# Order of the delta rule's 64x64 products, and how two convolution states are loaded and turned

## The chip, the cores and the metric

The kernel runs on one core of a Trainium2 chip. The metric is the device time of one execution, in microseconds (us). A core has five engines that work beside each other, each through its own list of instructions in order: TensorE (PE in the profile; its weight loads are PEld), VectorE (DVE), ScalarE (ACT), GpSimd (POOL) and SyncE (SP), whose queue issues all of this kernel's DMAs.

## What is computed

One decoder layer, for a prompt of 512 tokens and a group of 8 samples with one token each, with a model width of 1024. An input projection feeds two groups of heads beside each other: sparse attention and a gated delta rule. One output projection, a norm, a feed-forward network with a causal convolution of width 3, a second norm, a per-layer embedding and a third norm follow. The change touches the delta rule and the states of the two convolutions. Cut to these, the reference is:

```python
qkv, new_gbuf = causal_dwconv(h[..., C_GQKV:C_GA], gdn_buf, gdn_conv_w)
...
# gated_delta_chunked: chunks of 64 tokens, 8 heads of 64
X = lax.linalg.triangular_solve(A, rhs, left_side=True, lower=True)
val, kcd = X[..., :D], X[..., D:]
inner = jnp.einsum('nbhid,nbhjd->nbhij', q, k) * dec_incl
...
def step(S, xs):
    val_c, kcd_c, inner_c, qg_c, kend_c, gl = xs
    vn = val_c - jnp.einsum('bhcd,bhde->bhce', kcd_c, S)
    o = jnp.einsum('bhcd,bhde->bhce', qg_c, S) + jnp.einsum('bhij,bhje->bhie', inner_c, vn)
    S = S * jnp.exp(gl)[..., None, None] + jnp.einsum('bhcd,bhce->bhde', kend_c, vn)
    return S, o
...
hg, new_fbuf = causal_dwconv(up[..., :D_FF], ffn_buf, ffn_conv_w)
```

`causal_dwconv` puts the state's rows ahead of the new ones: 3 rows of 1536 features per sample for the delta rule, 2 rows of 2816 features per sample for the feed-forward network. Only the samples have such states; the prompt starts from zeros.

## The kernel before, in words

Activations lie feature-major: a tile holds 128 features as partitions and 520 tokens as columns (512 of the prompt, 8 samples), in two halves of 256 and 264 columns. A dense product (`product`, L299 to L307) goes over 8 tiles of the contraction with three matmuls each, since both operands are kept as a high and a low part: high weights by high activations (L303), low by high (L304), high by low (L307). `wtile` loads the weights into one of two buffers named raw (L192) and splits them, with ScalarE for the high part wh (L208) and DVE for the low one wl (L209). Those are the groups that fill the profile.

The delta rule's inputs come first. `gdn_tile` makes one tile of 128 of the 1536 features: a dense product into cb, then the convolution as a multiplication (L419) and pairs of multiply-adds on DVE, one for the prompt (L421), one for the samples (L422) with the state gst as operand. `vectors` (L332, L333) turns rows of parameters into per-feature columns at the first tile, and `conv_state` loads and turns a third of the state at every fourth one: a load of 24 rows (8 samples by 3) of 512 features (L352), four transposes on PE (L355) into one PSUM bank, a copy (L356).

The delta rule itself goes over four tiles tt of 128 tokens, each of two chunks c of 64. PE's array is used in quarters here: products of 64x64 whose contraction runs over one half of the partitions (rows) and whose result lands on one half of the output partitions (columns). A product's place is given by both halves.

- `gdn_pre(tt)` makes what needs no state: val (L667, rows c, columns c), kcd (L676, rows c, columns hp, the head's parity), and qk (L691, rows hp, columns c), each with 16 products, the last two with a PSUM bank per c and per hp.
- `gdn_step(tt, c)` goes from state to state: vn (L708), a subtraction per hp (L711), the new state's products S (L717), an addition (L719).
- `gdn_post(tt)` makes the output: o1 (L732, rows hp, columns c, a bank per hp) from queries and the state ahead of each chunk, o2 (L740), a norm over the heads, and transposes back to features (L751).

Within-chunk products kk (L536, L538) stand ahead of all that, in quarters that are 32 columns wide: four such tiles alternate.

The kernel keeps eight PSUM banks in four pools, `BANKS = dict(mm=2, pg=2, pc=1, pn=3)`. `gdn_pre` takes all of its banks from the two of pg; o1 and o2 use pn. The name of a tile in the profile is that of its PSUM tile: L732 shows as o, L691 as qk.

The program is written in stages whose order the text `ORDER` gives (G0, G1 ... are the delta rule's, D the input projections, F the feed-forward state, N0 and N1 the halves of the first norm, Y the output projection). A list scheduler then orders the instructions of each engine anew: it takes what it holds to be ready, earlier code first.

`ffn_state` is stage F. It stands among the last stages of attention, at some 375 to 397 us, and loads the feed-forward state in six loads of 16 rows (8 samples by 2) of up to 512 features (L1300), each turned by up to four transposes (L1303) and copied (L1304). Six tiles st16 and six PSUM banks of pg pass through it:

```python
for c0 in range(0, NFT, 4):
    n = min(4, NFT - c0)
    st = UV("st16", [16, 512])
    nc.sync.dma_start(st[:, :n * 128], I["state_ffn_conv"][0].rearrange("b r c -> (b r) c")[:, c0 * 128:(c0 + n) * 128])
```

Around it stand attention's last transposes (L940) and products (L947, L948), and the first norm of the first half: mean (L1176), subtraction (L1180), squares (L1182), variance (L1188).

Of the kernel before, what the change touches and what calls it, by code (L numbers as in the profile page):

```python
# [20 lines left out]
T = 512  # L21
# [80 lines left out]
def body(tc, nc, ctx, I, O, dbg=None):  # L102
# [51 lines left out]
    # activations that need a table, in an order that changes tables seldom  # L154
# [31 lines left out]
    # ---- dense products  # L186
# [47 lines left out]
    # ---- tokens to feature-major, in two f32r parts  # L234
# [13 lines left out]
    # the tensor engine's clock rises while the first rows come  # L248
# [39 lines left out]
    def by_halves(name, hv, tag, dt=F32, tiles=8):  # L288
        """tiles of one half, two to a slot"""
# [20 lines left out]
    def dense(specs, rh, rl, order=None, tags=("mm",), where=("w",), extra=None, ws=None, low=None):  # L310
        """specs: (parts, KT, M, evac); the first halves of all, then the second ones."""
# [13 lines left out]
    # per-feature vectors, by transposes of their rows  # L325
# [16 lines left out]
    # ---- delta-rule inputs: convolution, silu  # L342
# [4 lines left out]
    gst = UV("gst", [128, 12, 24])  # L347
    gstv = gst.rearrange("p j (b r) -> p j b r", r=3)

    def conv_state(hf):  # L350
        st = UV("st24", [24, 512])
        nc.sync.dma_start(st, I["state_gdn_conv"][0].rearrange("b r c -> (b r) c")[:, hf * 512:(hf + 1) * 512])  # L352
        ps = PS("gstT", "pn")
        for j in range(4):
            PE.transpose(ps[:, j * 24:(j + 1) * 24], st[:, j * 128:(j + 1) * 128], ident[:24, :24])  # L355
        V.tensor_copy(gst[:, hf * 4:(hf + 1) * 4, :], r3(ps[:, :96], 4))  # L356
# [4 lines left out]
    def gates():  # L361
# [6 lines left out]
        # both parts of the few columns in one operand  # L368
# [27 lines left out]
    def last_rows(rows, nt, outs, c0):  # L396
        """the last tokens' columns of nt tiles, turned and written"""
# [10 lines left out]
    def gdn_tile(j, ws=None):  # L408
# [6 lines left out]
        if j % 4 == 0:  # L415
            conv_state(j // 4)
# [17 lines left out]
    def l2norm(js):  # L434
        """rows of the heads scaled to unit length (queries with the softmax-like factor)"""
# [77 lines left out]
    # ---- within-chunk matrices, inverse of the unit triangular one  # L513
# [86 lines left out]
    # ---- delta rule of the samples, one token each  # L600
# [41 lines left out]
    # ---- delta rule over the chunks  # L642
# [5 lines left out]
    def gdn_pre(tt):  # L648
# [21 lines left out]
        p["kcd"] = U("kcd")  # L670
        for c in range(2):
            q = slice(c * 64, c * 64 + 64)
            pc = PS("kcd", "pg")
            for h in range(8):
                ht, hp = h // 2, h % 2
                PE.matmul(pc[hp * 64:hp * 64 + 64, ht * 64:ht * 64 + 64], kbg[q, h * 64:h * 64 + 64], TTt[q, h, :], start=True, stop=True)  # L676
            S.copy(p["kcd"][:, c * 256:c * 256 + 256], pc[:, :256])
# [906 lines left out]
```

## Time and profile before

| | us |
|---|---|
| median of 3 runs | 897.41 |
| lowest, highest | 895.09, 898.21 |
| span of the profiled execution | 892.7 |
| busy: PE, DVE, ACT, POOL | 859.2, 580.6, 426.6, 192.2 |
| DMA, mean | 96 GB/s |

The profiled execution is shown by its span alone, from the first to the last instruction; what lies around it is not shown. An engine's busy time is the union of its instructions' times. On PE a pass overlaps the next ones, so a short pause of PE hides in the end of a pass before, and two groups of matmuls are compared by the times at which passes start. An fp32 matmul shows as two passes, a matmul of the split type and a transpose as one. "Granted clock" is the share of TensorE's full clock of 2.4 GHz that it was granted: 1.00 is 2.4 GHz and 0.50 is 1.2 GHz.

### The profile page before, as it was taken

The numbers are of one execution on the slowest core, as the hardware profiler recorded it, in microseconds if no ns is written. First come the engines' busy times: TensorE is split into PE (matmuls) and PEld (weight loads), VectorE is DVE, ScalarE is ACT, GpSimd is POOL, SyncE is SP. The second block draws the span as 40 slices with busy tenths as digits, with TensorE's granted clock in tenths as the row PEclk, the third lists the DMA queues.
The fourth block names the chain that finished last, engine by engine and source line by source line (L and its number), as shares of the span: only waits on it lengthen the run. The fifth ranks groups of instructions, "written<-read, shape, count | busy, mean of one in ns | idle before, by whom it ended". The sixth has DMA issues, their size and how long they took to land.

```text
span 892.7 us, 19336 instructions
## 1 busy us (share of the span) xinstructions
PE 859.2 (96%) x7696; PEld 801.7 (90%) x7696; DVE 580.6 (65%) x1319; ACT 426.6 (48%) x940; POOL 192.2 (22%) x299
## 2 busy tenths in 40 slices
PE   8799999999998989999999999999999999998995
PEld 6779998988996758979899999999999999998984
DVE  4488996669869787779554553354543345577967
ACT  4364548323457885745644441244431244434744
POOL 0044040345404332206710000000000000005333
PEclk9899999999999999989999999999999999999998
DMA  8421331333237321333413333332343233352202
GB/s 270 116 67 37 104 91 53 109 96 84 68 98 231 94 79 30 104 101 107 118 48 96 96 105 88 94 90 88 88 117 95 60 87 117 93 162 78 95 1 96
DMA packets 137981, 85.92 MB, mean 96 GB/s; under 512 B 8186, under 2 KB 129708, under 8 KB 137844
## 3 DMA queue, kind: packets, MB, share of 16 engines
q1 hardware_dynamic: 137892, 84.70, 32.1%
q8 instruction: 60, 0.98, 0.4%
q14 instruction: 29, 0.24, 0.1%
HBM read 79.48 MB, written 7.36 MB: 97 GB/s over the span
## 4 chain that ended last, share of the span: by engine, by line
PE 81%; DMA 7%; DVE 7%; ACT 3%; issue 1%; POOL 1%; SPq 0%; DVEq 0%; POOLq 0%; ACTq 0%
PE mm L303 20%; PE mm L307 20%; PE mm L304 19%; PE PT L940 2%; DMA out_dram<-in_state_nsa_win_dram 2%; DMA praw<-in_ple_w_gate_dram 1%; DMA raw<-in_ffn_w_down_dram 1%; PE var L1188 1%; PE O L947 1%; PE O L948 1%; DVE wl L209 1%; PE S L904 1%; PE l L451 1%; DMA raw<-in_w_in_dram 1%; PE S L905 1%
## 5 line engine op out<-in xcount | busy, mean ns | idle before, releaser
L209 DVE TENSOR_TENSOR wl<-raw,wh 128x512 fp32r<-128x512 f32 x192 | 135.0, 705 | 147.4 <-ACT wh L208 146.0
L208 ACT CAST wh<-raw 128x512 fp32r<-128x512 f32 x200 | 121.5, 612 | 200.6 <-PE mm L307 151.1
L304 PE MATMUL mm<-x1h,wl 128*128 128x256 f32 (+1 forms) x704 | 198.3, 282 | 1.0 <-POOL wl L209 1.0
L307 PE MATMUL mm<-x1l,wh 128*128 128x256 f32 (+1 forms) x704 | 198.9, 283 | 0.0
L303 PE MATMUL mm<-x1h,wh 128*128 128x256 f32 (+1 forms) x704 | 198.5, 283 | 0.0
L304 PEld LDWEIGHTS mm<-x1h,wl 128*128 128x128 f32 x704 | 132.3, 188 | 1.3 <-POOL wl L209 1.2
L303 PEld LDWEIGHTS mm<-x1h,wh 128*128 128x128 f32 x704 | 132.3, 188 | 0.2 <-ACT wh L208 0.2
L307 PEld LDWEIGHTS mm<-x1l,wh 128*128 128x128 f32 x704 | 132.2, 188 | 0.1
L303 PE MATMUL mm<-xh,wh 128*128 128x256 f32 (+1 forms) x416 | 122.2, 294 | 0.0
L307 PE MATMUL mm<-xl,wh 128*128 128x256 f32 (+1 forms) x416 | 121.1, 291 | 0.4 <-DVE xl L273 0.4
L304 PE MATMUL mm<-xh,wl 128*128 128x256 f32 (+1 forms) x416 | 120.0, 288 | 0.0
L304 PE MATMUL mm<-hhl,wl 128*128 128x256 f32 (+1 forms) x352 | 99.9, 286 | 0.0
L303 PE MATMUL mm<-hhl,wh 128*128 128x264 f32 (+1 forms) x352 | 99.8, 286 | 0.0
L307 PE MATMUL mm<-hhl,wh 128*128 128x256 f32 (+1 forms) x352 | 99.6, 286 | 0.0
L303 PEld LDWEIGHTS mm<-xh,wh 128*128 128x128 f32 x416 | 79.7, 192 | 2.5 <-ACT xh L272 0.6
L307 PEld LDWEIGHTS mm<-xl,wh 128*128 128x128 f32 x416 | 79.7, 192 | 1.5 <-DVE xl L273 0.6
L304 PEld LDWEIGHTS mm<-xh,wl 128*128 128x128 f32 x416 | 79.6, 191 | 0.8 <-issue 0.5
L1343 POOL COPY last<-fcb 128x10 f32<-128x10 f32 x22 | 4.9, 224 | 309.6 <-ACT fcb L1331 298.1
L303 PEld LDWEIGHTS mm<-hhl,wh 128*128 128x128 f32 x352 | 66.8, 190 | 0.2
L304 PEld LDWEIGHTS mm<-hhl,wl 128*128 128x128 f32 x352 | 66.8, 190 | 0.2
L307 PEld LDWEIGHTS mm<-hhl,wh 128*128 128x128 f32 x352 | 66.4, 190 | 0.2
L1202 POOL TENSOR_SCALAR R<-R,vec 128x264 f32<-128x264 f32 (+1 forms) x40 | 31.0, 788 | 47.8 <-ACT x1h L1199 32.5
(442 smaller groups left out, 1866.3 us busy)
## 6 DMA issues: line engine op xcount, KB each, us to landing
raw<-in_ffn_w_up_dram SPq DMA_DIRECT2D x44, 512.0 KB
raw<-in_w_in_dram SPq DMA_DIRECT2D x26, 512.0 KB
raw<-in_w_out_dram SPq DMA_DIRECT2D x32, 256.0 KB
raw<-in_ffn_w_down_dram SPq DMA_DIRECT2D x16, 512.0 KB
pg<-in_cache_nsa_kv_dram SPq DMA_DIRECT2D x16, 256.0 KB
praw<-in_ple_w_gate_dram SPq DMA_DIRECT2D x8, 512.0 KB
raw<-in_ffn_w_down_dram SPq DMA_DIRECT2D x8, 384.0 KB
xr<-in_x_prompt_dram SPq DMA_DIRECT2D x4, 512.0 KB
```

Of the source, the lines that this page charges most:

```text
L208: both = (S.copy(th[:, :k1 - k0, :M], raw[:, k0:k1, :M]), low.tensor_tensor(tl[:, :k1 - k0, :M], raw[:, k0:k1, :M], th[:, :k1 - k0, :M], o ...
L209: low.tensor_tensor(tl[:, :k1 - k0, :M], raw[:, k0:k1, :M], th[:, :k1 - k0, :M], op=ALU.subtract))
L303: PE.matmul(o, hs[k], rh[hv][k], start=(k == ks[0]), stop=False)
L304: PE.matmul(o, ls[k], rh[hv][k], start=False, stop=False)
L307: PE.matmul(o, hs[k], rl[hv][k], start=False, stop=(k == ks[-1]))
L451: PE.matmul(ps, C("bd64"), sq[:, :T], start=True, stop=True)
L904: PE.matmul(ps[:, :wm], q_[:, ts_], kh[:, :wm], start=True, stop=False)
L905: PE.matmul(ps[:, :wm], q_[:, ts_], kl[:, :wm], start=False, stop=True)
L940: PE.transpose(pt[:, g4 * 128:g4 * 128 + 128], P[g4][:, st * 128:st * 128 + 128], ident)
L947: PE.matmul(po, VV[br][:, st, kv, :], pT_[0][:, :512], start=(br == 0 and st == 0), stop=False)
L948: PE.matmul(po, VV[br][:, st, kv, :], pT_[1][:, :512], start=False, stop=(br == 1 and st == tt))
L1202: G.tensor_scalar(r, r, b_, 1.0, op0=ALU.add, op1=ALU.mult)
```

## The change

Two edits, and comments taken out, which shift line numbers by up to 7.

- The loops of kcd, qk and o1 go over heads outside and chunks inside. For kcd that needs both banks at once, and the copies out of PSUM follow both.
- A helper `turned_rows` loads a state as rows of 128 features, so that sample, row and block of features together make the partitions: 288 rows for the delta rule, 352 for the feed-forward network. Up to three loads, three transposes into one PSUM bank, one copy. `conv_state` is called once, at the first tile. The columns of gst and fst stand in another order, so the multiply-adds read them with a stride.

```diff
-    gst = UV("gst", [128, 12, 24])
-    gstv = gst.rearrange("p j (b r) -> p j b r", r=3)
-
-    def conv_state(hf):
-        st = UV("st24", [24, 512])
-        nc.sync.dma_start(st, I["state_gdn_conv"][0].rearrange("b r c -> (b r) c")[:, hf * 512:(hf + 1) * 512])
-        ps = PS("gstT", "pn")
-        for j in range(4):
-            PE.transpose(ps[:, j * 24:(j + 1) * 24], st[:, j * 128:(j + 1) * 128], ident[:24, :24])
-        V.tensor_copy(gst[:, hf * 4:(hf + 1) * 4, :], r3(ps[:, :96], 4))
+    gst = UV("gst", [128, 288])
+    gstv = gst.rearrange("p (b r j) -> p j b r", b=8, r=3)
+
+    def turned_rows(out, src, n, name, tag):
+        st = UV(name, [128, 3, 128])
+        for a_ in range(0, n, 128):
+            m = min(128, n - a_)
+            nc.sync.dma_start(st[:m, a_ // 128], src[a_:a_ + m, :])
+        ps = PS(name + "T", tag)
+        for a_ in range(0, n, 128):
+            m = min(128, n - a_)
+            PE.transpose(ps[:, a_:a_ + m], st[:m, a_ // 128], ident[:m, :m])
+        V.tensor_copy(out, ps[:, :n])
+
+    def conv_state():
+        turned_rows(gst, I["state_gdn_conv"][0].rearrange("b r (j p) -> (b r j) p", p=128), 288, "gst", "pn")
...
         if not F:
             vectors()
-        if j % 4 == 0:
-            conv_state(j // 4)
+            conv_state()
...
-        for c in range(2):
-            q = slice(c * 64, c * 64 + 64)
-            pc = PS("kcd", "pg")
-            for h in range(8):
+        pcd = [PS("kcd", "pg") for c in range(2)]
+        for h in range(8):
+            for c in range(2):
+                q = slice(c * 64, c * 64 + 64)
                 ht, hp = h // 2, h % 2
-                PE.matmul(pc[hp * 64:hp * 64 + 64, ht * 64:ht * 64 + 64], kbg[q, h * 64:h * 64 + 64], TTt[q, h, :], start=True, stop=True)
-            S.copy(p["kcd"][:, c * 256:c * 256 + 256], pc[:, :256])
+                PE.matmul(pcd[c][hp * 64:hp * 64 + 64, ht * 64:ht * 64 + 64], kbg[q, h * 64:h * 64 + 64], TTt[q, h, :], start=True, stop=True)
+        for c in range(2):
+            S.copy(p["kcd"][:, c * 256:c * 256 + 256], pcd[c][:, :256])
...
         pq = [PS("qk", "pg"), PS("qk", "pg")]
-        for c in range(2):
-            t0 = tt * 128 + c * 64
-            for ht in range(4):
+        for ht in range(4):
+            for c in range(2):
+                t0 = tt * 128 + c * 64
                 for hp in range(2):
...
         po1 = [PS("o1", "pn"), PS("o1", "pn")]
-        for c in range(2):
-            q = slice(c * 64, c * 64 + 64)
-            t0 = tt * 128 + c * 64
-            for ht in range(4):
+        for ht in range(4):
+            for c in range(2):
+                q = slice(c * 64, c * 64 + 64)
+                t0 = tt * 128 + c * 64
                 for hp in range(2):
...
-        fst = UV("fst", [128, NFT, 16])
-        for c0 in range(0, NFT, 4):
...
-        FS["v"] = fst.rearrange("p j (b r) -> p j b r", r=2)
+        fst = UV("fst", [128, NFT * 16])
+        turned_rows(fst, I["state_ffn_conv"][0].rearrange("b r (j p) -> (b r j) p", p=128), NFT * 16, "fst", "pg")
+        FS["v"] = fst.rearrange("p (b r j) -> p j b r", b=8, r=2)
```

What the scheduler makes of it shows in the emitted order, at three places. First PE in `gdn_pre` of the first tile, where the products of qk stand between a matmul of another kind (DT) and the products of the state (S); qk_2227 and qk_2228 are the banks of hp 0 and 1, and the sources are the queries' and keys' tiles of the four ht. Before:

```order
L681 MATMUL DT_2222<-kbg_2171,cst 128x512
L691 MATMUL qk_2227<-qkv_1174,qkv_300 64x64
L691 MATMUL qk_2227<-qkv_1249,qkv_375 64x64
L691 MATMUL qk_2227<-qkv_1480,qkv_449 64x64
L691 MATMUL qk_2227<-qkv_1708,qkv_523 64x64
L691 MATMUL qk_2227<-qkv_1174,qkv_300 64x64
L691 MATMUL qk_2227<-qkv_1249,qkv_375 64x64
L691 MATMUL qk_2227<-qkv_1480,qkv_449 64x64
L691 MATMUL qk_2227<-qkv_1708,qkv_523 64x64
L307 MATMUL mm_2415<-xl_16_87,wh_2411 128x256
L717 MATMUL S_2490<-vn_2477,kend_2172 64x64 x8
```

Now, with kcd of the same stage above it (kcd_2186 and kcd_2187 are the banks of the chunks):

```order
L682 MATMUL kcd_2186<-TTa_947,kbg_2156 64x64 x8
L829 MATMUL kvT_2376<-cst,kvf_273_2313 128x128 x2
L845 MATMUL ntok_2387<-cst,kvf_273_2313 8x128
L682 MATMUL kcd_2187<-TTa_947,kbg_2156 64x64 x8
...
L688 MATMUL DT_2207<-kbg_2156,cst 128x512
L698 MATMUL qk_2212<-qkv_1167,qkv_301 64x64 x2
L698 MATMUL qk_2212<-qkv_1242,qkv_376 64x64 x2
L698 MATMUL qk_2212<-qkv_1465,qkv_450 64x64 x2
L698 MATMUL qk_2212<-qkv_1693,qkv_524 64x64 x2
L307 MATMUL mm_2400<-xl_16_87,wh_2396 128x256
L724 MATMUL S_2475<-vn_2462,kend_2157 64x64 x8
```

Within a bank of qk the two chunks now alternate (the x2), where the four ht of one chunk followed each other; the banks still come one after the other. The two banks of kcd still follow each other too.

Second, PE in `gdn_post` of the first tile, with two banks o per hp; Sst_2078 before and Sst_2063 now is the state ahead of the first chunk, Sst_2499 and Sst_2484 that ahead of the second. Before, first the last rows of chunk 0, then those of chunk 1 behind vn:

```order
L732 MATMUL o_311_2562<-Sst_2078,qkv_1708 64x64
L676 MATMUL kcd_2211<-TTa_946,kbg_2171 64x64 x8
...
L708 MATMUL vn_2536<-Sst_2499,kcd_2200 64x64 x8
L732 MATMUL o_310_2561<-Sst_2499,qkv_1174 64x64
L732 MATMUL o_311_2562<-Sst_2499,qkv_1174 64x64
L732 MATMUL o_310_2561<-Sst_2499,qkv_1249 64x64
L732 MATMUL o_311_2562<-Sst_2499,qkv_1249 64x64
```

Now:

```order
L739 MATMUL o_306_2546<-Sst_2063,qkv_1167 64x64
L739 MATMUL o_307_2547<-Sst_2063,qkv_1167 64x64
...
L715 MATMUL vn_2521<-Sst_2484,kcd_2185 64x64 x8
L739 MATMUL o_306_2546<-Sst_2484,qkv_1167 64x64
L739 MATMUL o_307_2547<-Sst_2484,qkv_1167 64x64
L739 MATMUL o_306_2546<-Sst_2063,qkv_1242 64x64
L739 MATMUL o_307_2547<-Sst_2063,qkv_1242 64x64
L739 MATMUL o_306_2546<-Sst_2484,qkv_1242 64x64
L739 MATMUL o_307_2547<-Sst_2484,qkv_1242 64x64
```

Six of the eight products of chunk 0 have moved from ahead of vn to behind it, where both states and both hp alternate.

Third, SP's queue at the feed-forward state (st before, fst now). Before:

```order
L1247 DMA xr_5413<-in_x_prompt_dram 128x2x128
L1300 DMA st_951_5775<-in_state_ffn_conv_dram 16x512
L192 DMA raw_5733<-in_w_out_dram 128x4x128
...
L192 DMA raw_5972<-in_w_out_dram 128x4x128
L1300 DMA st_953_5783<-in_state_ffn_conv_dram 16x512
L1300 DMA st_955_5791<-in_state_ffn_conv_dram 16x512
L1300 DMA st_957_5799<-in_state_ffn_conv_dram 16x512
L1300 DMA st_959_5807<-in_state_ffn_conv_dram 16x512
L1300 DMA st_961_5815<-in_state_ffn_conv_dram 16x256
```

Now:

```order
L1254 DMA xr_5398<-in_x_prompt_dram 128x2x128
L355 DMA fst_5760<-in_state_ffn_conv_dram 128x128 x2
L355 DMA fst_5760<-in_state_ffn_conv_dram 96x128
L192 DMA raw_5718<-in_w_out_dram 128x4x128
```

All loads of the state now stand where the first one stood; six loads of weights lay between the first and the second. On PE the three transposes stand where the first four of 22 stood.

## Rows read from the trace of the kernel before

**Rows 1.** The page: span, and busy time of each engine with its share and instructions

```profile
span 892.7 us, 19336 instructions
PE 859.2 (96%) x7696; PEld 801.7 (90%) x7696; DVE 580.6 (65%) x1319; ACT 426.6 (48%) x940; POOL 192.2 (22%) x299
```

**Rows 2.** Windows (us; busy us and instructions per engine; PEclk; DMA share; GB/s)

```profile
200.00:265.00 65.00, 65.00 (x862) 59.44 (x861) 53.19 (x108) 29.48 (x70) 22.99 (x29) 1.00 0.29 81
265.00:300.00 35.00, 31.71 (x244) 25.23 (x243) 31.32 (x122) 29.72 (x97) 16.97 (x23) 1.00 0.54 165
```

**Rows 3.** Timeline of PE (start, length, instructions, idle before and releaser), qk

```profile
168.95 0.96 PE L691 MATMUL qk<-qkv,qkv 64*64 64x64 f32 x16
169.84 0.39 PE L307 MATMUL mm<-xl,wh 128*128 128x256 f32 x1
```

**Rows 4.** Timeline of PE, kcd

```profile
162.87 0.63 PE L676 MATMUL kcd<-TTa,kbg 64*64 64x64 f32 x15
163.43 0.44 PE L822 MATMUL kvT<-cst,kvf 128*128 128x128 f32 x2
```

**Rows 5.** Windows, instructions of kk alone (PE, PEld, DVE)

```profile
72.95:74.10 1.15, 0.98 (x64) 0.82 (x64) 0.03 (x1) 1.00 0.00 0
```

**Rows 6.** Timeline of PE, the third group of gst

```profile
84.29 0.42 PE L355 MATMUL gstT<-cst,st 24*128 24x24 f32 x4
84.64 0.39 PE L303 MATMUL mm<-xh,wh 128*128 128x256 f32 x1
84.86 0.28 PE L304 MATMUL mm<-xh,wl 128*128 128x256 f32 x1
84.98 0.28 PE L307 MATMUL mm<-xl,wh 128*128 128x256 f32 x1
```

**Rows 7.** Timeline of PE, the first tile's vectors and state

```profile
29.84 0.29 PE L332 MATMUL vec<-cst,vr 114*128 114x114 f32 x1 [4.06 <-DMA vr<-in_ffn_conv_w_dram]
...
30.90 0.59 PE L355 MATMUL gstT<-cst,st 24*128 24x24 f32 x4 [0.45 <-DMA st<-in_state_gdn_conv_dram]
31.42 0.59 PE L307 MATMUL mm<-xl,wh 128*128 128x264 f32 x1
31.81 0.41 PE L303 MATMUL mm<-xh,wh 128*128 128x256 f32 x1
```

**Rows 8.** Timeline of SP's queue at the same place

```profile
29.09 0.30 SPq L352 DMA_DIRECT2D st<-in_state_gdn_conv_dram  x1
29.50 0.40 SPq L192 DMA_DIRECT2D raw<-in_w_in_dram  x1
```

**Rows 9.** Groups by line: busy us, mean ns, idle before with releaser

```profile
L1303 PE MATMUL fstT<-cst,st 16*128 16x16 f32 x22 | 2.5, 236 | 1.4 <-DMA st<-in_state_ffn_conv_dram 1.4
```

**Rows 10.** Timeline of PE around the feed-forward state

```profile
384.75 1.03 PE L940 MATMUL PT<-cst,P 128*128 128x128 f32 x8
...
391.17 0.63 PE L1303 MATMUL fstT<-cst,st 16*128 16x16 f32 x8 [1.40 <-DMA st<-in_state_ffn_conv_dram]
...
400.67 3.29 PE L1188 MATMUL var<-lsq,cst 128*128 128x256 f32 x14 [0.83 <-ACT lsq L1182]
```

**Rows 11.** Timeline of SP's queue there

```profile
374.73 0.41 SPq L1300 DMA_DIRECT2D st<-in_state_ffn_conv_dram  x1
376.92 10.73 SPq L192 DMA_DIRECT2D raw<-in_w_out_dram  x6
387.74 2.31 SPq L1300 DMA_DIRECT2D st<-in_state_ffn_conv_dram  x5
```

**Rows 12.** Windows at the low clock (columns as in rows 2)

```profile
30.60:37.30 6.70, 6.40 (x31) 6.38 (x32) 2.67 (x7) 2.90 (x6) 0.45 (x1) 0.50 0.62 102
392.40:399.10 6.70, 6.70 (x27) 4.84 (x25) 4.29 (x11) 2.82 (x7) 0.00 (x0) 0.50 0.28 82
```

**Rows 13.** Timeline of DVE, the first norm

```profile
398.21 2.74 DVE L1180 TENSOR_TENSOR R<-R,mu 128x256 f32<-128x256 f32 x8 [0.47 <-PE mu L1176]
```

**Rows 14.** Groups by line of DVE, 155 to 265 us

```profile
L711 DVE TENSOR_TENSOR vn<-vb,vn 64x256 f32<-64x256 f32 x16 | 6.7, 417 | 4.0 <-PE vn L708 3.8
```

More of the change, by code (lines that the diff above doesn't have):

```diff
@@ L670, in gdn_pre @@
         p["kcd"] = U("kcd")
-        for c in range(2):
-            q = slice(c * 64, c * 64 + 64)
-            pc = PS("kcd", "pg")
-            for h in range(8):
-                ht, hp = h // 2, h % 2
-                PE.matmul(pc[hp * 64:hp * 64 + 64, ht * 64:ht * 64 + 64], kbg[q, h * 64:h * 64 + 64], TTt[q, h, :], start=True, stop=True)
-            S.copy(p["kcd"][:, c * 256:c * 256 + 256], pc[:, :256])
+        pcd = [PS("kcd", "pg") for c in range(2)]
+        for h in range(8):
+            for c in range(2):
+                q = slice(c * 64, c * 64 + 64)
+                ht, hp = h // 2, h % 2
+                PE.matmul(pcd[c][hp * 64:hp * 64 + 64, ht * 64:ht * 64 + 64], kbg[q, h * 64:h * 64 + 64], TTt[q, h, :], start=True, stop=True)
+        for c in range(2):
+            S.copy(p["kcd"][:, c * 256:c * 256 + 256], pcd[c][:, :256])
         rr = kbg
@@ L1295, in ffn_state @@
     def ffn_state():
-        fst = UV("fst", [128, NFT, 16])
-        for c0 in range(0, NFT, 4):
-            n = min(4, NFT - c0)
-            st = UV("st16", [16, 512])
-            nc.sync.dma_start(st[:, :n * 128], I["state_ffn_conv"][0].rearrange("b r c -> (b r) c")[:, c0 * 128:(c0 + n) * 128])
-            ps = PS("fstT", "pg")
-            for j in range(n):
-                PE.transpose(ps[:, j * 16:(j + 1) * 16], st[:, j * 128:(j + 1) * 128], ident[:16, :16])
-            V.tensor_copy(fst[:, c0:c0 + n, :], r3(ps[:, :n * 16], n))
-        FS["v"] = fst.rearrange("p j (b r) -> p j b r", r=2)
+        fst = UV("fst", [128, NFT * 16])
+        turned_rows(fst, I["state_ffn_conv"][0].rearrange("b r (j p) -> (b r j) p", p=128), NFT * 16, "fst", "pg")
+        FS["v"] = fst.rearrange("p (b r j) -> p j b r", b=8, r=2)
         nc.sync.dma_start(O[11][0, :, 0, :], I["state_ffn_conv"][0, :, 1, :])
```

## The prediction

> **What bounds the kernel now.** I began with the page [rows 1]: TensorE (PE) is busy for 859.2 of a span of 892.7 us. So a saving counts where it shortens PE's own sequence, a wait of PE, or a stretch at the low clock. Next came the timelines of PE around the places that the diff touches: the delta rule (160 to 265 us), the three groups of transposes of the first convolution state (31, 67 and 84 us), and the transposes of the second one (387 to 397 us); last the queue of the loads and the windows with the clock. The profile gives a span, 892.7 us, 4.7 below the median of the three runs (897.41); I make the sum against the span and add the same 4.7.
>
> In the delta rule PE is busy for 65.0 of 65 us and VectorE (DVE) for 53.2 [rows 2]: PE is the bound, and passes that run closer together shorten the stage. Each fp32 product of 64x64 is two passes in the trace.
>
> **The 64x64 products.** The reader should compare start times, since a pass lasts some 0.22 us whatever runs beside it. A qk block has 16 passes and takes 0.89 us until the next matmul starts [rows 3]: its products keep to one half of the contraction rows, and four in a row to one half of the output partitions. A kcd block, whose products keep to one half of the rows and alternate between the halves of the output, has 15 passes in 0.56 us, some 30 ns at a steady pace [rows 4]. A block of kk, where four tiles of the array alternate, has 64 passes in 0.98 us, the last pass's own 0.22 included: 12 ns per pass [rows 5]. So alternating two tiles comes close to halving the price, and four tiles halve it again.
>
> What the emitted order makes of it, group by group:
> - **kcd: 0.** The bank of chunk 0 is still filled by eight products, and only then the bank of chunk 1. Within each the contraction half stays fixed, as before. The alternation of four doesn't come about here.
> - **qk: -2.2 us.** Each bank still has its eight products together, but in it the chunks now alternate, so it becomes a block of kcd's kind: 16 passes for 0.59 us (0.56 and one step more) instead of 0.89. That saves 0.30, times 8 blocks 2.4. In four of the eight, products of the state already overlap a few passes, so I take 2.2; the bounds are 0 and 2.4.
> - **o1: -1.5 us.** Here all four tiles do alternate. 128 passes at 30 ns are 3.8 us, at 12 to 15 ns (kk's pace, half of whose tiles are narrower) 1.5 to 1.9: a gain of 2.3 at most. Some twelve of the 64 products stand in pairs away from the rest and gain nothing, so 1.5; the bounds are 0 and 2.3.
> - **Crossings: +0.6 us.** By the emitted order, PE goes between 64x64 products and others 66 times, 60 before. Such a crossing costs a part of a step: after small products the second full matmul starts 0.22 us behind the first, where later ones are 0.12 apart [rows 6]. Six times 0.1; the bounds are 0 and 1.2.
>
> On these rows the Trainium skill speaks against the change. In "TensorE: Matmul & The Clock Gate", Part 3, "The mechanism", it says that a weight load overlaps matmuls in flight only when the row group differs, and that matmuls never leave their order. In qk the row group stays fixed for a whole bank, so by that rule the 2.2 of qk are 0; o1 alternated row groups already and would gain 0 too. Rows 4 disagree for two column halves, since kcd runs with its row group fixed. I go by the rows and keep the rule as a rival below.
>
> **The first convolution state.** Three loads of 24 rows and twelve transposes become three loads of rows of 128 and three transposes, all at the first tile.
> - The groups at 67 and 84 us go. The four that start at 84.29 push the next matmul to 84.64 [rows 6]: 0.35 each, **-0.7 us**. Their copies on DVE are covered by a PE that has no gap there.
> - At the start PE stands for 4.06 us, until the rows of the vectors land, and again 0.45 for the state's load [rows 7], issued at 29.09, 0.41 before the next load on its queue [rows 8]. Now three loads are issued there, so the last lands some 0.8 later. The tile's last matmul (0.39 from 31.42 to 31.81 [rows 7]) now runs in that wait, by the emitted order, and three transposes stand for four. I take **+0.4 us**; the bounds are 0 and 0.8. The weights behind on the queue come 0.8 later too; they are for the tile after next, and the 48 matmuls of the next one cover that.
>
> **The second convolution state.** Six loads and 22 transposes become three and three.
> - The 22 keep PE busy for 2.5 us [rows 9], 2.2 without the ends of last passes, which other work overlaps. Three transposes of 128 columns cost 0.3, by the eight in 1.03 at 384.75 [rows 10]. **-1.9 us.**
> - The first load is issued at 374.73, the other five only at 387.74, because output weights ahead of them on the queue wait for buffers [rows 11]. That is the 1.40 us that PE stands before 391.17 [rows 10]. All three now stand where the first one stood, 12 us ahead of use, and their issue (three times 0.41) ends before 376.92, when the queue goes on anyway. **-1.4 us.** The five issues, 2.31 us of queue time ahead of more weights, go too; I cost that at nothing, since ScalarE's casts pace those loads.
> - Soon after that gap the granted clock is at its lower level, 1.2 of 2.4 GHz, for the 6.7 us from 392.4 to 399.1 [rows 12]. The gap of 4.06 us at the start has the same sequel, from 30.6 to 37.3 [rows 7, 12]. With the gap before 391.17 gone, the likeliest is that the low stretch goes. It is worth between 0 and 3.4 us (half of 6.7). Part of it comes back as waiting: the norm behind it is paced by eight subtractions on DVE (2.74 us from 398.21 [rows 13]) and by ScalarE's squares, for which PE already stands 0.83 us at 400.67 [rows 10]. I take the middle, **-1.7 us**.
>
> Sum: -2.2 - 1.5 + 0.6 - 0.7 + 0.4 - 1.9 - 1.4 - 1.7 = **-8.4 us**: a span of 884.3, a time of **889.0**.
>
> **Rivals.**
> - *The low clock stays.* The new order puts the norm's first products between the last transposes, and another short wait there keeps it. Without the 1.7: 890.7. For it: the work in that stretch is thin (27 matmuls in 6.7 us). Against: the gap ahead of it is gone.
> - *The gain is given back where DVE is the bound.* From 265 to 300 us DVE is busy for 31.3 of 35 and PE for 31.7 [rows 2]. If DVE can't start that stage earlier, the 3.1 of the delta rule turn into waits of PE: 892.1. Against: between 200 and 265 DVE has 12 us of slack.
> - *Products overlap only across row groups* (the rule above). As a mechanism of this kernel, qk and o1 keep their pace, and 3.7 are missing: 892.7. Against: rows 4 and 5.
> - *Slower: PE waits for the state in o1.* Before, the pairs of chunk 0 ran when their state was there, and those of chunk 1 after the next one. Now the first pair of chunk 1 stands ahead of three pairs of chunk 0, and all that is behind on PE waits with them. If the second state is late, PE stands for what lies between the states: three DVE steps of 0.42 [rows 14] and two groups of 16 passes at 30 ns, 2.3 us. By rows 7 and 12 such a gap can be followed by a low clock, which takes 3.4 more. Four tiles at 5.7 are 22.8, and o1's 1.5 goes too: 913.3. It decides from 1.7 us per tile: the other terms sum to -6.9. Against: the emitted order puts the pairs of chunk 1 behind vn of the same state, which needs it as well.
> - *The change doesn't do what it says*: true for kcd, and in the sum.
>
> **How the numbers follow.** The main case gets 0.51, the low clock that stays 0.21, the gain given back 0.14, the rule of row groups 0.08, the late state 0.06. A measurement of this kernel can tell about 0.3%, 2.7 us, from no change, so faster means below 894.7. The first four cases lie there, each with a spread of some 3 us (the bounds of qk, o1, crossings and clock, and an order that is new on every engine). I leave 0.02, 0.02, 0.04 and 0.02 of them to no change, and of the late state 0.02 to no change and 0.04 to slower, with 0.01 of the given-back case beside it. That makes 0.83 faster, 0.12 the same and 0.05 slower. The range goes from 885.0 (the clock's 3.4 and o1's 2.3 in full, crossings at 0, less a little) to 895.5 (the two 892 cases with their spread); it leaves out the late state and the ends of the others.
>
> **What would show it.** Right: qk blocks of 16 passes in 0.6 us; o1 at under 20 ns per pass; kcd unchanged; no wait for a load of the second state; a granted clock of 1.00 around 390 to 400 us; a slightly longer wait of PE at 30 us. Wrong: a gap of PE of over 2 us in the delta rule that a state ended, or waits of PE from 265 to 300 us that have grown by what the stage before saved; then the sum fails although each row is right.

## The result and the profile after

| | kernel before | changed kernel |
|---|---|---|
| median of the runs | 892.7 us (8 runs, 891.27 to 898.21) | 899.06 us (8 runs, 893.65 to 900.62) |
| ratio | 1 | 1.0053 (95%: 1.0031 to 1.0075) |
| span of the profiled execution | 892.7 us | 897.9 us (time 899.93) |
| mean granted clock of the runs | 0.987 to 0.989 (runs beside the experiments) | 0.985 |

The change made the kernel about half a percent slower; the forecast was 889.0, faster. The three runs that it started from lay high: five more gave 891.3 to 893.3, and the runs beside the experiments had medians of 890.8 to 892.0, with 2.1 us around the span instead of 4.7. The forecast is best read as a ratio, 889.0 / 897.41 = 0.991. The measured ratio, 1.0053, is the estimate on record, here and below, and not the quotient of the medians; that is 1.0071 and lies inside the interval.

The page of the changed kernel, span and busy time of the engines, as in [rows 1]:

```profile
span 897.9 us, 19269 instructions
PE 854.6 (95%) x7668; PEld 796.9 (89%) x7668; DVE 579.7 (65%) x1312; ACT 426.6 (48%) x940; POOL 187.9 (21%) x299
```

PE works 4.6 us less than in [rows 1], and the span is 5.2 longer: PE waits more, and the question is where.

Timeline of PE, a block of qk and the matmul behind it, to set beside [rows 3], and the core of a block of o1:

```profile
170.04 0.68 PE L698 MATMUL qk<-qkv,qkv 64*64 64x64 f32 x16
170.65 0.39 PE L307 MATMUL mm<-xl,wh 128*128 128x256 f32 x1
...
176.38 0.52 PE L739 MATMUL o<-Sst,qkv 64*64 64x64 f32 x22
```

Groups by line, PE, 155 to 300 us: first the kernel before, then the changed one:

```profile
L691 PE MATMUL qk<-qkv,qkv 64*64 64x64 f32 x128 | 7.7, 224 | 0.0
L732 PE MATMUL o<-Sst,qkv 64*64 64x64 f32 x128 | 7.6, 227 | 0.0
```

```profile
L739 PE MATMUL o<-Sst,qkv 64*64 64x64 f32 x128 | 5.9, 229 | 0.0
L698 PE MATMUL qk<-qkv,qkv 64*64 64x64 f32 x128 | 5.8, 223 | 0.0
```

A qk block takes 0.61 us until the next matmul instead of 0.89, its passes start (0.68 - 0.22) / 15 = 31 ns apart, and o1's (0.52 - 0.22) / 21 = 14 ns. The busy time of the two falls by 1.9 and 1.7 us. The array did what the forecast said.

Timeline of PE around the feed-forward's state and the first norm, beside [rows 10] (brackets: the wait before, and what ended it):

```profile
389.01 0.46 PE L359 MATMUL fstT<-cst,fst 128*128 128x128 f32 x3
...
394.14 0.50 PE L954 MATMUL O<-PTh,VV 128*128 128x512 f32 x1 [1.79 <-ACT PTh L952]
394.48 0.59 PE L1183 MATMUL mu<-acc,cst 128*128 128x256 f32 x2
...
395.55 0.60 PE L947 MATMUL PT<-cst,P 128*128 128x128 f32 x4
...
396.22 0.60 PE L947 MATMUL PT<-cst,P 128*128 128x128 f32 x4
...
401.43 1.02 PE L1195 MATMUL var<-lsq,cst 128*128 128x256 f32 x4
402.10 0.58 PE L955 MATMUL O<-PTl,VV 128*128 128x512 f32 x1
406.12 1.16 PE L1022 MATMUL cmpo<-csT,VCb 128*128 128x256 f32 x4 [3.44 <-DVE mix L1023]
```

and in the kernel before:

```profile
392.31 0.57 PE L947 MATMUL O<-PTh,VV 128*128 128x512 f32 x1
...
395.21 1.06 PE L940 MATMUL PT<-cst,P 128*128 128x128 f32 x4
...
397.11 1.05 PE L1176 MATMUL mu<-acc,cst 128*128 128x256 f32 x2
```

The state's rows are no longer waited for, and three transposes do the work of 22. But PE now waits 1.79 us for PTh (the copy of transposed probabilities that an attention product O needs) and 3.44 us ahead of cmpo. Not all of the 5.2 us between the two profiles arises here: by the start times of the same dense matmuls the changed kernel stands 2.0 us later at 380 us, 4.1 at 510 and 4.9 at 860. Of the first 2.0, 1.4 are there by 105 us, and 1.6 come between 300 and 380 us, where PE waits longer for other loads (up to 1.11 us at 316); the delta rule between gives 1.0 back.

ScalarE (ACT) and VectorE (DVE) of the changed kernel at the same place:

```profile
391.58 0.62 ACT L208 CAST wh<-raw 128x512 fp32r<-128x512 f32 x1 [1.50 <-DMA raw<-in_w_out_dram]
392.98 0.62 ACT L197 CAST wh<-raw 128x512 fp32r<-128x512 f32 x1 [0.78 <-DMA raw<-in_w_out_dram]
393.51 1.07 ACT L952 CAST PTh<-PT 128x512 fp32r<-128x512 f32 x2
...
402.49 0.47 ACT L164 ACTIVATE rstd<-var,eps 128x256 f32<-128x256 f32 x1 [1.56 <-PE var L1195]
402.99 0.75 ACT L960 COPY pos<-O 64x256 f32<-64x256 f32 x2
```

```profile
403.77 0.85 DVE L962 TENSOR_TENSOR mix<-O,pos 64x256 f32<-64x256 f32 x2 [3.20 <-ACT pos L960]
404.65 0.69 DVE L198 TENSOR_TENSOR wl<-raw,wh 128x512 fp32r<-128x512 f32 x1
405.25 0.48 DVE L1204 SCALAR_TENSOR_TENSOR R<-R,vec,rstd 128x256 f32<-128x256 f32 x1
405.65 0.75 DVE L1023 TENSOR_TENSOR mix<-cmpo,mix 128x256 f32<-128x256 f32 x2
```

and ACT of the kernel before:

```profile
390.80 0.62 ACT L197 CAST wh<-raw 128x512 fp32r<-128x512 f32 x1 [1.09 <-DMA raw<-in_w_out_dram]
391.32 0.58 ACT L945 CAST PTh<-PT 128x512 fp32r<-128x512 f32 x1
...
399.43 0.75 ACT L953 COPY pos<-O 64x256 f32<-64x256 f32 x2 [0.35 <-PE O L948]
...
404.00 0.47 ACT L164 ACTIVATE rstd<-var,eps 128x256 f32<-128x256 f32 x1 [0.27 <-PE var L1188]
```

The 1.79: both casts PTh stand behind two casts of output weights, which wait for their transfers. The 3.44: pos, the copy of the attention's last product, stood ahead of rstd, the first step of the norm's 1/std; now it stands behind it, and rstd waits for the norm's last column sum. DVE's mix waits for pos, and PE for mix. ACT's order alone is little of it: the product that pos copies ends at 402.68, and pos starts at 402.99, 0.3 us later. Another 1.0 us is DVE's order, where a weight's wl and a step of the norm stand between the two kinds of mix (404.65 to 405.65). The rest is the chain pos, mix, mix itself, behind which PE stands, since its last attention product comes behind the norm's last column sum. PE's order explains that: mu, the norm's first sum, stood behind the last transposed probabilities, and now stands ahead of the last two blocks of them, so that the attention ends among the norm's products.

Windows of the changed kernel (columns as in [rows 2]) for the clock, beside [rows 12]:

```profile
392.40:399.10 6.70, 4.28 (x20) 2.95 (x21) 6.33 (x15) 4.62 (x11) 0.00 (x0) 1.00 0.28 80
407.20:410.40 3.20, 3.20 (x15) 2.95 (x14) 3.20 (x11) 0.38 (x2) 0.00 (x0) 0.50 0.17 48
```

The low stretch at 392 us went, but PE worked only 4.28 of those 6.70 us, and another one came behind the wait of 3.44. Over the whole span the mean granted clock is 0.985 in both profiles, so the clock doesn't explain what lies between them.

### The profile page after: what moved, and what is told of

It reads as the page before. It is cut to its first block, busy times and chain, and to the rows that moved or that the text cites. A ratio compares the mean times of both kernels' runs of the same rounds, so it can differ in the third digit from the quotient of the medians.

```text
span 897.9 us, 19269 instructions
## 1 busy us (share of the span) xinstructions
PE 854.6 (95%) x7668; PEld 796.9 (89%) x7668; DVE 579.7 (65%) x1312; ACT 426.6 (48%) x940; POOL 187.9 (21%) x299
## 4 chain that ended last, share of the span: by engine, by line
PE 73%; DMA 11%; DVE 9%; ACT 4%; issue 2%; POOL 1%; SPq 1%; DVEq 0%; POOLq 0%; ACTq 0%
PE mm L303 18%; PE mm L307 18%; PE mm L304 18%; DMA out_dram<-in_state_nsa_win_dram 2%; DMA raw<-in_w_out_dram 1%; DVE wl L209 1%; PE PT L947 1%; DMA raw<-in_ffn_w_down_dram 1%; DMA raw<-in_ffn_w_up_dram 1%; DMA praw<-in_ple_w_gate_dram 1%; ACT wh L208 1%; DMA xr<-in_x_prompt_dram 1%; DMA pg<-in_cache_nsa_kv_dram 1%; PE var L1195 1%; PE O L954 1%
## 5 line engine op out<-in xcount | busy, mean ns | idle before, releaser
L1331 ACT COPY fcb<-mm 128x256 f32<-128x256 f32 (+1 forms) x44 | 16.5, 377 | 53.2 <-PE mm L307 52.6
```

The costliest lines, as they stand in the source:

```text
L1331: S.copy(cb[:, 2 + c0:2 + c1], ps[:, :c1 - c0])
```

## Experiments: the parts alone

My theory A was that the reorder pays and the loss comes from the order of instructions around the second state; the rival B that the delta rule loses what its passes save.

**only_order** (the three loop orders alone), **qk_o1_only** (without kcd):

```diff
...
-        for c in range(2):
...
-            for ht in range(4):
+        for ht in range(4):
+            for c in range(2):
...
```

> The kernel before with the three new loop orders of the 64x64 products and nothing else; both convolution states are loaded as before. Theory A (the reorder pays what its rows show, 1.7 us in qk and 1.6 us in o1, part of it given back where DVE is waited for, and the loss of the whole change comes from elsewhere): 0.5 to 3.5 us under the kernel before. Theory B (the loss comes from the delta rule: what the passes save is lost in crossings, in waits between 200 and 265 us, and in what follows at a shifted time): 0 to 3 us over the kernel before.

> The kernel before with the loop orders of qk and o1 alone; kcd and both states as before. Theory A (kcd's two PSUM tiles, held together over sixteen passes, delay the tiles behind them in the same pool of two and give back part of what qk and o1 gain): 1.5 to 3 us under the kernel before. Theory B (what the passes save turns into waits for VectorE in the recurrence, with or without kcd): within 1 us of the kernel before, as only_order.

Measured: only_order 0.9999 (0.9983 to 1.0015), qk_o1_only 0.9993 (0.9977 to 1.0010). No change, with kcd or without: the loss comes from elsewhere, as theory A of only_order said, and the gain is nearer to theory B's. By the intervals at most 1.5 to 2 us of the 3.6 us less busy time arrive; the profiles resolve it better. Timeline of PE, the same two groups of matmuls on either side of the delta rule, in the kernel before and in the changed one:

```profile
149.88 1.04 PE L615 MATMUL sT<-cst,qkv 128*8 128x128 f32 x8
289.78 1.07 PE L1070 MATMUL pmean<-pg,cst 128*32 128x256 f32 x16 [0.29 <-ACT KT L1060]
```

```profile
151.32 1.04 PE L621 MATMUL sT<-cst,qkv 128*8 128x128 f32 x8
290.22 1.07 PE L1077 MATMUL pmean<-pg,cst 128*32 128x256 f32 x16 [0.31 <-ACT KT L1067]
```

That is 139.9 us against 138.9. Between the same dense matmuls at 150 and 300 us all fourteen profiles with the new loops of qk and o1 are 0.9 to 1.2 us shorter than the first profile of the kernel before, and the five others with the old loops lie within 0.1 of it. So about 1 us of the 3.6 arrives.

Matching the same matmuls in the timelines of before and only_order shows where the rest goes: the difference is -0.4 us at 150, -3.6 at 196 and -1.5 from 275 us on. The 3.6 hold a wait of 0.83 us at 194 us, ahead of vn, that had gone. At 205 us only_order has a new one, behind dense products:

```profile
204.95 0.28 PE L307 MATMUL mm<-xl,wh 128*128 128x256 f32 x1
206.37 0.59 PE L718 MATMUL S<-vn,kend 64*64 64x64 f32 x13 [1.13 <-DVE vn L712]
```

The state's product S waits for DVE's subtraction. The recurrence goes PE, DVE, PE, DVE, and a PE that arrives earlier waits for DVE; the rest, 1 us, goes in smaller steps up to 275 us, among them a wait of 0.6 us for a copy on ACT that the kernel before doesn't have; I did not trace it further.

**only_first_state**, **order_and_first_state**, **qk_o1_and_first_state**:

```diff
...
-        if j % 4 == 0:
-            conv_state(j // 4)
+            conv_state()
...
```

> The kernel before with the delta rule's convolution state as rows of 128 and nothing else. Theory A (the two groups of transposes at 67 and 84 us go, 0.7 us, and the price is the longer copy and a later DVE, which the product of the gates' sums waits for at 49 us, 2.50 us where the kernel before had 1.36 us, with a low-clock stretch of 3.4 us behind it that costs 1.4 us): 0.5 to 2 us over the kernel before, with that wait over 2 us. Theory B (the wait at 49 us is a chance of the one profiled run): 0.7 us under the kernel before.

> The whole change without its last part: loop orders and the delta rule's state as changed, the feed-forward's state as before. ScalarE's order around the first norm is then that of the kernel before. Theory A (the last part alone brings the loss): 0 to 4 us under the kernel before. Theory B (the loss comes from the delta rule): 2 to 5 us over the kernel before.

> The kernel before with the loop orders of qk and o1 and the delta rule's state as rows of 128; kcd and the feed-forward's state as before. Theory A (each part pays what the rows show once the rest is away): 1.5 to 3 us under the kernel before, faster than both. Theory B (what the passes save turns into waits in the recurrence, and the state's groups were hidden): within 1.2 us of the kernel before.

Measured: 1.0025 (1.0008 to 1.0042) alone, 0.9992 (0.9975 to 1.0009) with all orders, 1.0002 (0.9986 to 1.0018) with qk and o1. Alone this edit made the kernel slower, by 0.7 to 3.7 us, and on top of the loop orders it did nothing, so its sign isn't settled. One of its terms is: between dense matmuls at 62 and 105 us all twelve profiles with the new state are 0.7 to 0.8 us shorter than the kernel before, and the seven others lie within 0.01 of it. The wait at 49 us, on which theory A put a loss, was 1.36 us in only_first_state, as in the kernel before, and 1.89 with a low-clock stretch behind it in a second profile of the kernel before (before_again, below): it belongs to the execution, and A fell there. What matters is that everything but the last part (order_and_first_state) shows no loss.

**only_second_state**:

```diff
...
-        for c0 in range(0, NFT, 4):
...
+        turned_rows(fst, I["state_ffn_conv"][0].rearrange("b r (j p) -> (b r j) p", p=128), NFT * 16, "fst", "pg")
```

> The kernel before with the feed-forward's convolution state as rows of 128 and nothing else. Theory A (the nineteen transposes and the wait for their rows go, but ScalarE's order around the first norm becomes the one of the whole change: the copy of the last attention product stands behind the first step of the norm's 1/std, so that the last VectorE addition, and with it TensorE, waits about 3 us at 400 us, and a new low-clock stretch follows): 2 to 5 us over the kernel before. Theory B (the loss comes from the delta rule and this edit pays as forecast): 3 to 5 us under the kernel before.

Measured: 1.0055 (1.0038 to 1.0072), 4.9 us. Theory A; this one edit is the loss, since without it there is none and alone it has all of it. Timeline of its PE and the window behind (clock 0.50), from an execution that was the slowest of the seven:

```profile
392.51 0.50 PE L959 MATMUL O<-PTh,VV 128*128 128x512 f32 x1 [1.60 <-ACT PTh L957]
...
404.47 2.08 PE L1027 MATMUL cmpo<-csT,VCb 128*128 128x256 f32 x4 [3.44 <-DVE mix L1028]
```

```profile
403.80:410.40 6.60, 5.93 (x21) 5.33 (x22) 6.18 (x20) 2.44 (x8) 1.12 (x3) 0.50 0.15 42
```

## Experiments: the order around the norm

These add order edges between instructions of one engine, and no work. **copy_ahead** puts rstd behind pos on ACT; **norm_held** puts mu behind the last PT on PE and the norm's first subtraction behind the last PTl on DVE; **second_state_norm_held** does the same to only_second_state:

```diff
...
+        if n_ == 0:
+            after(ln, L["pos"])      # copy_ahead
...
+            after(mu, L["pt"])       # norm_held
...
+                after(sub, L["ptl"]) # norm_held
```

> The whole change, and one order added on ScalarE: the copy of the last attention product (pos) is issued ahead of the first step of the first norm's 1/std, instead of behind it. Theory A (the wait of 3.44 us at 400 us is ScalarE's order: the copy stands behind a step that waits for the last column sum): the copy starts when its product ends, about 2 us earlier, and the time falls by about 2 us from the whole change's, to 2 to 3.5 us over the kernel before; the wait of about 1.6 us behind PTh at 391 us stays. Theory B (the wait is set by the late products themselves, not by the copy): under 0.5 us of it goes.

> The whole change, and two orders added: the first norm's column sum (mu) stands behind the last transposes of the attention's probabilities on TensorE, and the norm's first subtraction stands behind the last PTl on VectorE, as both did in the kernel before. Theory A (the loss is the first norm pulled ahead of the attention's last products, once the feed-forward state's groups no longer hold it back): the wait of 3.44 us at 400 us goes, the transposes' 1.9 us and part of the 1.4 us for the state's rows stay gained: 2 to 5 us under the kernel before. Theory B (the loss comes from the state's long rows or their transfers themselves, not from the order): 3 to 5 us over the kernel before, as the whole change.

> The kernel before with the feed-forward's state as rows of 128, and the two orders of norm_held; loop orders and first state as before. Theory A (the edit itself pays what its rows show, about 1.9 us of transposes and up to 1.4 us of waiting, once the norm stands where it stood): 1.5 to 4 us under the kernel before. Theory B (it costs by itself): 3 us or more over the kernel before.

copy_ahead: 1.0039 (1.0022 to 1.0057), 3.5 us, the upper end of theory A; the interval overlaps that of the whole change, so a gain isn't shown. pos starts at 399.53 in its trace, 0.03 us behind its product. The wait fell by 1.26 us where A expected about 2, most of it by DVE's order, which changed too: one mix now follows the other (400.31 and 401.19):

```profile
401.67 1.13 PE L1022 MATMUL cmpo<-csT,VCb 128*128 128x256 f32 x4 [2.18 <-DVE mix L1023]
```

norm_held: 1.0046 (1.0031 to 1.0061), once more 1.0037 (1.0022 to 1.0053); a miss: theory A expected a gain, and the time is B's. The wait ahead of cmpo is gone, and the loss is not:

```profile
391.65 0.50 PE L954 MATMUL O<-PTh,VV 128*128 128x512 f32 x1 [1.72 <-ACT PTh L952]
...
398.93 1.13 PE L1199 MATMUL var<-lsq,cst 128*128 128x256 f32 x4 [0.51 <-ACT lsq L1193]
```

second_state_norm_held: 1.0029 (1.0009 to 1.0048), half the loss of only_second_state and still no gain; between the theories, and the two intervals overlap.

**three_groups**, in both states each 128 rows with a PSUM tile and a copy of their own:

```diff
...
+            ps = PS(name + "T", tag)
             PE.transpose(ps[:, :m], st[:m, a_ // 128], ident[:m, :m])
+            V.tensor_copy(out[:, a_:a_ + m], ps[:, :m])
```

> The whole change, but each transposed group of 128 rows has a PSUM tile and a VectorE copy of its own, so that the feed-forward state takes three tiles of the pool that the first norm's sums also use (the kernel before: six, the whole change: one). Theory A (the groups held the norm back by holding those two buffers): the norm's first sum is emitted later than in the whole change and earlier than in the kernel before, and the time lies between, 0.5 to 4 us over the kernel before. Theory B (the number of groups does not matter, the length of the rows does): as the whole change, 4 to 5.5 us over the kernel before.

Measured: 1.0090 (1.0060 to 1.0119), the slowest of all. mu did move, to ahead of the last block only, as A said of the order; the time did not follow. The wait ahead of cmpo is longer, because DVE now puts all eight steps of the norm between the two kinds of mix:

```profile
401.25 3.25 DVE L1204 SCALAR_TENSOR_TENSOR R<-R,vec,rstd 128x256 f32<-128x256 f32 x8
404.89 2.08 PE L1022 MATMUL cmpo<-csT,VCb 128*128 128x256 f32 x4 [5.60 <-DVE mix L1023]
```

**casts_behind** holds four weights' casts behind PTh and PTl of the attention's last blocks, on norm_held; **old_state_casts_behind** does so with the old second state, without norm_held's edges:

```diff
...
+    BEHIND = {(1, 6): 0, (0, 2): 1, (0, 3): 2, (0, 4): 3}
...
+            for b_, e_ in zip(both, hold):
+                after(b_, e_)
...
```

> norm_held, and on ScalarE and VectorE the two parts of four output weights (tiles 6, 2, 3 and 4) stand each behind the cast and subtraction of one of the last four blocks of probabilities, instead of some ahead of them. Theory A (the wait of 1.7 us behind PTh at 390 us is ScalarE waiting in order for a weight tile still in transfer; it took the place of the wait for the state's rows, so that the shorter transposes saved nothing): that wait falls under 0.5 us, and the time to 0 to 3 us under the kernel before. Theory B (the weights' transfers set the pace of this stage): the wait reappears at the products after 400 us, and the time stays 3 to 5 us over the kernel before.

> order_and_first_state (the feed-forward's state as before, in six groups), with the casts of the same four weights held behind as in casts_behind. Theory A (the state's rows of 2 KB are waited for in this place, 1.45 us, and hidden only as long as ScalarE is late as well): the wait for the rows stays, and the time is within 1.5 us of order_and_first_state, 2.5 us under to 1 us over the kernel before; casts_behind is then 0 to 2 us faster than this one. Theory B (the long rows cost by themselves): this one is 2 us or more faster than casts_behind.

Measured: 1.0058 (1.0037 to 1.0079) and 1.0052 (1.0036 to 1.0068). The wait behind PTh went, and came back ahead of the norm's sums, so theory B held for casts_behind, with a loss of 5.2 us where it had 3 to 5. The profiled execution was the fastest of its six, so the line shows where the wait went and not what it costs:

```profile
395.09 0.70 PE L1206 MATMUL var<-lsq,cst 128*128 128x256 f32 x2 [1.69 <-ACT lsq L1200]
```

The old state with the same casts is as slow (its trace has the clock low for 13.7 us from 391 us), so neither theory foresaw it: holding the casts costs by itself, and with them held, long rows or old groups make no difference.

## Experiments: were the transposes on the path?

**transposes_back** is norm_held with nineteen transposes of a constant, whose result nothing reads, and the attention product behind each group (o_) held behind it; **norm_held_again** its base and **before_again** the control:

```diff
...
+                for j in range(9 + st):
+                    b_ = PE.transpose(L["back"][:, (9 * st + j) * 16:(9 * st + j) * 16 + 16], ident[:16, :128], ident[:16, :16])
+                    after(b_, L["pt"])
...
+                after(o_, b_)
...
```

> norm_held, with nineteen transposes of 16 rows of a constant put back on TensorE (nine behind the last but three blocks of transposed probabilities, ten behind the next); nothing reads them. They are work that this kernel does on top. Theory A (the transposes that the change took away were hidden: TensorE waits here for the chain from the probabilities' casts through the norm's sums, and 1.9 us less work is 1.9 us more waiting): the wait of 1.7 us at 390 us shrinks by most of their duration, and the time is within 1 us of norm_held. Theory B (they were on the path, as the forecast's term of 1.9 us has it): 1.5 to 2.5 us slower than norm_held.

> norm_held once more, on the chip of transposes_back: both theories need it as the base of that comparison; 3 to 5 us over the kernel before if the first measurement holds, under 2 us if it was a chance of that chip.

> The kernel before, unchanged, as a control: a ratio of 1.000 within 0.002, and a profile taken on this chip. If the waits between 380 and 430 us are those of the first profile (1.40, 0.83, 0.42 and 0.99 us), they belong to the kernel and not to one execution; the low-clock stretch behind them may differ.

Measured on one chip: 1.0014 (0.9998 to 1.0030), 1.0037 and 0.9998 (0.9979 to 1.0017). With more work the kernel is not slower, if anything 2 us faster. Timeline of its PE:

```profile
389.65 0.72 PE L952 MATMUL back<-cst 16*128 16x16 f32 x9
...
391.17 0.79 PE L952 MATMUL back<-cst 16*128 16x16 f32 x10
392.31 0.50 PE L960 MATMUL O<-PTh,VV 128*128 128x512 f32 x1 [0.35 <-ACT PTh L958]
```

The wait for PTh is 0.35 instead of 1.72: the transposes fill it. That is theory A's mechanism, though the time lies some 2 us below norm_held_again, outside A's 1 us, and the two intervals overlap. In this order of the norm the forecast's 1.9 us are not on the path. The control adds that the wait which I had put down to the rows' transfer has more than one holder. The same transposes, in the second profile of the kernel before:

```profile
391.53 0.64 PE L1303 MATMUL fstT<-cst,st 16*128 16x16 f32 x8 [1.30 <-DVE PTl L946]
```

The clock differed as well. transposes_back has none of the low stretches that norm_held_again shows behind its waits (1.71 us at 390, then 0.75 and 0.96 at 423 to 425); but it has a wait of 0.97 us at 424 as well, and no low stretch behind that one. Its window, then two of norm_held_again:

```profile
390.00:402.00 12.00, 9.47 (x51) 6.17 (x50) 10.16 (x23) 8.33 (x22) 0.00 (x0) 1.00 0.32 95
```

```profile
392.30:395.50 3.20, 3.13 (x11) 2.66 (x12) 1.58 (x4) 1.59 (x3) 0.00 (x0) 0.50 0.36 99
426.50:429.70 3.20, 3.20 (x16) 3.20 (x16) 2.45 (x2) 2.26 (x7) 3.20 (x4) 0.50 0.52 147
```

So I asked whether useless work in a wait keeps the clock up in general, with the same edit on other kernels: **before_filled**, **order_first_filled**, **qk_o1_filled**.

> The kernel before with the same nineteen constant transposes and nothing else. Theory A: 1 to 3 us under the kernel before, without a low-clock stretch behind 392 us (6.83 us in both profiles of the kernel before). Theory B: no change, or up to 1 us slower.

> order_and_first_state with the nineteen constant transposes of transposes_back on top, between the last blocks of transposed probabilities and the wait for the state's rows (1.45 us at 390 us). Theory A (a wait there costs twice, once itself and once by a low-clock stretch behind it, 6.83 us in that run's profile, which half-speed makes 3.4 us; useless work in the wait prevents the second): the stretch behind 390 us goes or halves, 1 to 3.5 us under the kernel before, faster than both kernels. Theory B (the low clock there does not depend on this wait): as order_and_first_state or up to 1 us slower.

> qk_o1_only with the same nineteen constant transposes. Theory A: 1.5 to 3.5 us under the kernel before. Theory B: within 1 us of it, as qk_o1_only.

Measured: 1.0019 (0.9996 to 1.0041), 1.0039 (1.0020 to 1.0058), 0.9997 (0.9976 to 1.0017). It doesn't: where the old groups already fill the wait, more filling costs or does nothing. In the profile of order_first_filled the low stretch did go (the mean clock from 388 to 402 us is 1.00), and the time rose all the same. Theory A fell, and no version here beats the kernel before by more than its interval.

## Why the prediction was wrong

- **kcd 0, qk -2.2, o1 -1.5: right as busy time** (0, -1.9, -1.7). The rival by the rule of row groups is out: a qk block would have kept its 0.89 us, and it takes 0.61, though its row group is fixed within a bank. The rule is that of the Trainium skill ("TensorE: Matmul & The Clock Gate", Part 3, "The mechanism"), by which a weight load overlaps matmuls in flight only when the row group differs; this trace disagrees.
- **The rival of the gain given back was right in kind, with a chance of 0.14.** About 1.0 of the 3.1 us arrives. I put the given-back time at 265 to 300 us; most of it had gone by 265, and the wait of 1.13 us behind vn is in the recurrence itself. "VectorE has 12 us of slack" is an average, and the step that PE waited for had none. The late state in o1, my slower rival, didn't occur.
- **First state -0.7 + 0.4:** the -0.7 is in every profile (0.7 to 0.8). The 0.4 is smaller than what two executions of the kernel before differ by at that place (0.9 us at 62 us), so no profile shows it.
- **Second state, transposes -1.9: the step that failed.** The rows showed them busy, and I took busy for on the path. transposes_back shows that work of that size there costs nothing. With the next term I forecast 3.3 us less from this edit; alone it measured 4.9 more.
- **The wait for rows -1.4:** failed with it. The wait went, and 1.6 to 1.8 us behind PTh took its place in every kernel with the new state but three_groups and those that held the casts or filled the wait. "ScalarE's casts pace those loads" was my reason to cost the queue at nothing; the reverse reading, that casts waiting for loads stand ahead of PTh on ACT, was the one that counted. It could be read before: PTh's cast of 391.32 to 391.90 stood behind a cast that had waited 1.09 us for its load, and the product at 392.31 needs it. By an estimate from these rows, landed rows would have let that product start at 391.9, 0.4 us earlier and not 1.4, with the transposes or without.
- **Not in the sum at all:** the new order around the norm, on PE, ACT and DVE, with its wait of 3.44 us. I compared PE and the load queue, and ACT only for their sake. In the words of the forecast, "an order that is new on every engine" was spread, where it brought the longest single wait. What it costs isn't 3.44: norm_held has no such wait and is still 3.3 to 4.1 us over the kernel before.
- **Clock -1.7:** the stretch at 392 went, and others came. Over the runs, span times (1 - mean granted clock) is 13.5 us in the changed kernel and 9.4 to 11.5 in the kernel before on the chips of the experiments; as an estimate, up to 2 to 4 lost where 1.7 were to be gained. It can't be the whole loss: in only_second_state the same figure is 10.6 us, against 10.0 in the kernel before beside it.

Left open: what makes the edit of the second state cost 4.9 us, and why norm_held stays 3.3 to 4.1 us over the kernel before. That the gain failed is shown, and so is which edit brings the loss; which of its waits the loss consists of is not, and no run excludes that the long rows or their transfers cost by themselves. In its two profiles the stretch from the block of PT at 384 us to the second half's mu is no longer than in order_and_first_state (39.0 and 38.7 us against 40.3), and its mean clock explains some 2 us, by the estimate above. Why the scheduler lets mu ahead was not settled either. The old groups and the norm's sums share a PSUM pool of two, and three_groups moved mu as that would have it; that is an argument, not a proof.

## What to carry to other kernels

Before counting removed work as gain, look for the wait right behind it: work that fills a wait for another engine is free, and its removal only uncovers the wait. When a list scheduler orders the program, compare the emitted order on every engine that takes part in the stage, ScalarE as well, and look at each instruction that has moved behind one that waits. The length of the new wait is not yet its price: taking out the one of 3.44 us gave no gain beyond the intervals. And read a saving in a recurrence at the engine that answers each step, not at the stage's mean slack.

## Not expected of the hardware

- Passes of 64x64 products that alternate only between the two column halves, with one row half, start 31 ns apart in the new qk block; with all four tiles, in o1, 14 ns.
- Low-clock stretches move between executions of one program: the kernel before had one at 52 us in one of its two profiles (window 52.0 to 55.2 us at 0.50 in before_again, none in the first) and one at 392 us in both. One profile therefore prices such a stretch only roughly:

```profile
393.30:399.90 6.60, 6.60 (x25) 4.62 (x24) 4.57 (x13) 3.25 (x9) 0.00 (x0) 0.50 0.28 82
52.00:55.20 3.20, 3.20 (x17) 3.20 (x16) 2.15 (x5) 2.13 (x3) 1.81 (x2) 0.50 0.02 7
```
